# Attention with TensorE's order written out by hand instead of left to the scheduler

## The chip, the cores and the metric

One core of a Trainium2 chip runs the whole kernel. The metric is the device time of one execution in microseconds (us), from the first to the last instruction of the program and what little lies around them. The engines are TensorE (PE: matmuls and transposes; PEld is its loading of weights), VectorE (DVE), ScalarE (ACT), GpSimd (POOL) and SyncE (SP, which here issues the DMAs). Each engine works through its own list of instructions in a fixed order; an instruction whose input is not there yet holds up everything behind it on that engine.

## What is computed

One layer of a trunk with 1024 frames of 1024 channels, in float32 (the matmul operands are split in a high and a low part, and a product is three matmuls, so that it keeps the precision). Only the attention matters here:

```python
x = x + 0.5 * swiglu(rmsnorm(x))
h = rmsnorm(x)
[a | q | k | v | gate logits] = h @ w_in
yA = gMLP spatial gating of gelu(a)
# yB: stick-breaking attention, 16 heads of 64 channels, strictly causal, blocks of 128 frames
z = q_block @ k[:kend].T * scale                     # kend = 128 * (block + 1)
log_keep = where(causal, -softplus(z), 0)
log_w = log_sigmoid(z) + reverse_cumsum(log_keep) - log_keep
out = where(causal, exp(log_w), 0) @ v
m = sigmoid(gA) * (yA @ W_A) + sigmoid(gB) * (yB @ W_B)
x = x + m @ W_out
x = x + 0.5 * swiglu(rmsnorm(x)); y = rmsnorm(x)
```

## The kernel before

The program runs in stages: a first feed-forward block, the attention with its projections (its first scores start at 740.1 us, its last product with v at 1266.7 us), the gated branch `gmlp` with the gates and the merge, and a second feed-forward block. Within a stage most of the order is not written in the code: a scheduler places the instructions of all engines at build time, by its own estimate of when each would be ready. The lists it makes are fixed; nothing is reordered on the chip. A block `manual_schedule(engines={PE})` keeps TensorE's instructions in the order of the code; in the attention before the change only the first projection of v stands in such a block.

**The work of one head** (`head`, line 601 on; 16 heads, two to a pair). The head has eight blocks of 128 queries, b = 0 to 7. For each block TensorE makes the scores `z` in PSUM (tag `p0`, three buffers) from `q` and from `kh` and `kl`, the two parts of k, in pieces of at most 512 keys; ScalarE makes two sigmoids of them, `kp` (what is kept) and `bt`; GpSimd masks the diagonal (`affine_select`); VectorE runs a reversed product scan over the whole row of `kp` (128 to 1024 elements, longer for later blocks); GpSimd, and for the second half of long rows VectorE, multiplies `bt` by it. Two blocks make a step c = 0 to 3. For a step TensorE transposes the weights in groups of two key blocks (`tr`, PSUM tag `p2`, two buffers: 1, 2, 3 and 4 groups in steps 0 to 3), ScalarE and VectorE split each group into a high and a low part (`wt`, by `split`), and TensorE multiplies them with v into `av` (the first product of a group needs the high part, the second the low one). After steps 1 and 3 ScalarE copies `av` to `y` and two DMAs write it out.

**The projections.** `proj_v` makes v for four heads (a quad) in products of 24 matmuls of 256 columns (`pv`); `proj_qk` makes q and k for a pair, each in two halves of 24 matmuls of 512 columns (`pj`). Both use PSUM tag `p1`, two buffers. ScalarE and VectorE split the results. The parts of k are then copied to the other 64 partitions by DMA, and scores need the original and the copy. The tiles of q, `kh` and `kl` have three buffers each, two of which a pair uses. Weights come by DMA into `raw`, ScalarE makes the high part (`wf`, line 56) and VectorE the low part (line 57).

The code calls the two heads of a pair, then the projections for the next; the scheduler moves the projections between the steps of the heads as their buffers allow. The first four products of gate logits (`GAT = 4`, dictionary `ga`) come after the attention in the code, and their tiles are of a pool that is open by then, so the scheduler uses them in the last pair of heads.

Of the kernel before, what the change touches and what calls it, by code (L numbers as in the profile page):

```python
# [24 lines left out]
GAT = 4  # L25
# [7 lines left out]
class Kernel:  # L33
# [525 lines left out]
    def attention(self, ap, ydram):  # L559
        nc, w_in = self.nc, self.a["w_in"][0]  # L560

        def proj_v(quad):
            units = [self.load_cols(w_in, C_VV + quad * 256, kt0, 4, 256) for kt0 in (0, 4)]
            vt = []
            for t in range(NT):
                if quad == 0 and t and self.pending:
                    self.pending.pop(0)()
                half, c = t // 4, (t % 4) * P
                ps = self.psum("p1", "pv")
                for k in range(NK):  # L570
                    wh, wl = units[k // 4]
                    hh, hl = (self.h[half][part][:, k, c:c + P] for part in range(2))
                    self.mm3(ps[:, :256], hh, hl, wh[:, k % 4, :], wl[:, k % 4, :], k == 0, k == NK - 1)
                pool = ap if quad % 2 else self.gp
                v = pool.tile([P, 4, 2, HD], F32R, tag="v", bufs=8, name="v")
                self.split(v[:, :, 0, :], v[:, :, 1, :], ps[:, :256].rearrange("p (h d) -> p h d", h=4))
                vt.append(v)
            return vt

        def proj_qk(pair):  # L580
            lo, hi = slice(0, HD), slice(HD, P)
            kl = [ap.tile([P, S], F32R, tag="kl", bufs=3, name="kl") for _ in range(2)]
            q = [ap.tile([P, S], F32R, tag="q", bufs=3, name="q") for _ in range(2)]
            kh = [ap.tile([P, S], F32R, tag="kh", bufs=3, name="kh") for _ in range(2)]
            wh, wl = self.load_cols(w_in, C_Q + pair * P)
            for half in range(2):
                cs = slice(half * HALF, (half + 1) * HALF)
                ps = self.proj_t("p1", wh, wl, half)
                for e, (own, other) in enumerate(((lo, hi), (hi, lo))):
                    self.split(q[e][own, cs], q[e][other, cs], ps[own, :])  # L590
            wh, wl = self.load_cols(w_in, C_K + pair * P)
            for half in range(2):
                cs = slice(half * HALF, (half + 1) * HALF)
                ps = self.proj_t("p1", wh, wl, half)
                for e, (own, other) in enumerate(((lo, hi), (hi, lo))):
                    self.split(kh[e][own, cs], kl[e][own, cs], ps[own, :])
                    for k in (kh[e], kl[e]):
                        nc.sync.dma_start(out=k[other, cs].bitcast(F32), in_=k[own, cs].bitcast(F32))
            return [(q[e], kh[e], kl[e]) for e in range(2)]

        def head(hd, q, kh, kl, vt):
            hq = hd % 4
            for c in range(4):
                if c % 2 == 0:
                    av = self.psum("p3", "av")
                wts = []
                for b in (2 * c, 2 * c + 1):
                    kend = (b + 1) * P
                    kp = ap.tile([P, S], F32, tag="kp", bufs=KPB, name="kp")
                    bts = []  # L610
                    for s0 in range(0, kend, HALF):
                        n = min(HALF, kend - s0)
                        z = self.psum("p0", "z")
                        nc.tensor.matmul(z[:, :n], lhsT=q[:, b * P:(b + 1) * P], rhs=kh[:, s0:s0 + n], start=True, stop=False)
                        nc.tensor.matmul(z[:, :n], lhsT=q[:, b * P:(b + 1) * P], rhs=kl[:, s0:s0 + n], start=False, stop=True)
                        bt = ap.tile([P, HALF], F32, tag="bt", bufs=BTB, name="bt")
                        nc.scalar.activation(kp[:, s0:s0 + n], z[:, :n], AF.Sigmoid, scale=-(HD ** -0.5))
                        nc.scalar.activation(bt[:, :n], z[:, :n], AF.Sigmoid, scale=HD ** -0.5)
                        bts.append(bt)
                    dk = kp[:, b * P:kend]  # L620
                    db = bts[-1][:, (b % 4) * P:(b % 4 + 1) * P]
                    for d, fill in ((dk, 1.0), (db, 0.0)):
                        nc.gpsimd.affine_select(d, d, pattern=[[-1, P]], compare_op=ALU.is_gt, fill=fill, base=0, channel_multiplier=1)  # L623
                    rev = kp[:, 0:kend][:, ::-1]
                    nc.vector.tensor_tensor_scan(rev, rev, rev, 1.0, op0=ALU.mult, op1=ALU.bypass)  # L625
# [6 lines left out]
                for j0 in range(0, 2 * c + 2, 2):  # L632
# [3 lines left out]
                    for jj in range(2):  # L636
                        j = j0 + jj
                        for bb in range(2):
                            if diag and jj == 1 and bb == 0:
                                continue  # L640
# [23 lines left out]
        for pair in range(npair):  # L664
# [4 lines left out]
            if pair + 1 < npair:  # L669
                qk[pair + 1] = proj_qk(pair + 1)  # L670
# [250 lines left out]
```

## Time and profile before

| | us |
|---|---|
| median of three runs (2529.93 to 2532.69) | 2530.52 |
| the profiled execution's own time | 2532.02 |
| its span, first to last instruction | 2530.3 |
| busy: TensorE | 2455.8 (97%) |
| busy: VectorE | 1675.4 (66%) |
| busy: ScalarE | 1045.0 (41%) |
| busy: GpSimd | 341.9 (14%) |
| mean granted clock of TensorE | 0.984 of full speed |

Busy times of different engines overlap. A busy TensorE need not be a fast one: at half the clock its matmuls take longer and it counts as busy all the same, so the granted clock of a stretch has to be read beside its busy time. The profiled execution took 1.7 us more than its span.

### The profile page before, as it was taken

To read this page: it belongs to the slowest core of one execution; us is meant where nothing else is said; L and a number is where in the kernel's file an instruction comes from. 1 tells how busy PE (TensorE), PEld (TensorE's weight loads), DVE (VectorE), ACT (ScalarE), POOL (GpSimd) and SP (SyncE) were. 2 spreads that over 40 slices of the span, in tenths; PEclk is the share of its full clock that TensorE was granted. 3 is DMA by queue.
4 is the path that set the end of the run, shared out by engine and by line. 5 is a ranking of instruction groups with operands and counts; after the bars stand their busy time and mean duration, and the time that the engine had idled before them with its cause. 6 is when DMAs were issued, how large, how long until landed. Compare 5 with 4: busy or idle time off the path is not lost.

```text
span 2530.3 us, 33327 instructions
## 1 busy us (share of the span) xinstructions
PE 2455.8 (97%) x12268; PEld 2082.9 (82%) x12268; DVE 1675.4 (66%) x2581; ACT 1045.0 (41%) x1994; POOL 341.9 (14%) x508
## 2 busy tenths in 40 slices
PE   7999999999999999999999999999989999999998
PEld 6888888788788888888888988888868888887886
DVE  5777777565747888876666556145757777874655
ACT  6333333354546666665522222232343333333444
POOL 4000000000314444443300000000130000000002
PEclk9999999999999999999999999999999999999999
DMA  5553553785412222221121122133345535547753
GB/s 151 178 171 126 177 176 122 266 290 172 157 51 51 67 51 67 51 67 55 51 53 49 54 76 88 53 101 133 122 147 177 172 130 178 171 138 254 265 174 133
DMA packets 257636, 326.73 MB, mean 129 GB/s; under 512 B 15680, under 2 KB 172864, under 8 KB 257472
## 3 DMA queue, kind: packets, MB, share of 16 engines
q1 hardware_dynamic: 257472, 324.60, 39.7%
q8 instruction: 96, 1.57, 0.3%
q14 instruction: 68, 0.56, 0.1%
HBM read 231.74 MB, written 84.41 MB: 125 GB/s over the span
## 4 chain that ended last, share of the span: by engine, by line
PE 88%; DVE 5%; DMA 3%; issue 1%; ACT 1%; POOL 1%; SPq 0%; DVEq 0%; POOLq 0%; ACTq 0%
PE pd L170 7%; PE pd L172 7%; PE pd L171 7%; PE pj L67 7%; PE pj L68 7%; PE pj L69 7%; PE pb L172 5%; PE pb L171 5%; PE pb L170 5%; PE av L649 3%; PE pv L67 2%; PE pv L68 2%; PE pv L69 2%; PE tr L642 2%; PE pe L171 2%; PE pe L172 2%
## 5 line engine op out<-in xcount | busy, mean ns | idle before, releaser
L154 ACT CAST wf<-raw 128x512 fp32r<-128x512 f32 x280 | 167.2, 620 | 255.7 <-PE pd L172 106.6
L155 DVE TENSOR_TENSOR wf<-raw,wf 128x512 fp32r<-128x512 f32 x264 | 180.2, 702 | 122.9 <-ACT wf L154 122.4
L67 PE MATMUL pj<-h,wf 128*128 128x512 f32 x640 | 255.4, 399 | 5.6 <-DVE q L74 5.6
L68 PE MATMUL pj<-h,wf 128*128 128x512 f32 x640 | 254.7, 398 | 0.0
L69 PE MATMUL pj<-h,wf 128*128 128x512 f32 x640 | 254.0, 397 | 0.6 <-DVE wf L57 0.6
L625 DVE TENSOR_TENSOR_SCAN kp<-kp 128x128 f32<-128x128 f32 (+7 forms) x128 | 178.8, 1406 | 38.4 <-POOL kp L623 36.9
L57 DVE TENSOR_TENSOR wf<-raw,wf 128x1024 fp32r<-128x1024 f32 x88 | 109.5, 1245 | 135.0 <-ACT wf L56 135.0
L154 ACT CAST wf<-ws 128x512 fp32r<-128x512 f32 x176 | 108.0, 622 | 202.2 <-DVE ws L163 106.5
L56 ACT CAST wf<-raw 128x1024 fp32r<-128x1024 f32 x88 | 92.6, 1053 | 219.8 <-PE pj L68 122.2
L67 PE MATMUL pv<-wf,h 128*128 128x256 f32 x512 | 146.9, 289 | 6.9 <-DVE h L74 4.8
L67 PEld LDWEIGHTS pj<-h,wf 128*128 128x128 f32 x640 | 122.8, 192 | 31.5 <-DVE q L74 7.1
L68 PE MATMUL pv<-wf,h 128*128 128x256 f32 x512 | 147.4, 288 | 0.2 <-DVE wf L57 0.2
L69 PE MATMUL pv<-wf,h 128*128 128x256 f32 x512 | 147.1, 288 | 0.0
L629 POOL TENSOR_TENSOR bt<-bt,kp 128x512 f32<-128x512 f32 (+4 forms) x128 | 127.9, 1002 | 138.1 <-DVE kp L625 108.9
L69 PEld LDWEIGHTS pj<-h,wf 128*128 128x128 f32 x640 | 122.4, 191 | 26.0 <-DVE wf L57 1.2
L68 PEld LDWEIGHTS pj<-h,wf 128*128 128x128 f32 x640 | 122.7, 192 | 24.1
L115 POOL TENSOR_TENSOR xn<-x,gain 128x512 f32<-128x512 f32 x12 | 17.2, 1434 | 896.7 <-DVE x L513 601.1
L170 PE MATMUL pb<-T,wf 128*128 128x512 f32 x352 | 137.6, 391 | 0.0
L171 PE MATMUL pb<-T,wf 128*128 128x512 f32 x352 | 137.2, 390 | 0.0
L172 PE MATMUL pb<-T,wf 128*128 128x512 f32 x352 | 137.0, 389 | 0.0
L171 PE MATMUL pd<-wf 128*128 128x512 f32 x344 | 134.4, 392 | 1.3 <-DVE wf L155 1.3
L170 PE MATMUL pd<-wf 128*128 128x512 f32 x344 | 126.7, 401 | 8.3 <-ACT wf L154 8.2
(217 smaller groups left out, 6573.2 us busy)
## 6 DMA issues: line engine op xcount, KB each, us to landing
raw<-in_ff_w_down_dram SPq DMA_DIRECT2D x66, 512.0 KB, 6.2
raw<-in_w_in_dram SPq DMA_DIRECT2D x56, 512.0 KB, 4.1
raw<-in_ff_w_gate_dram SPq DMA_DIRECT2D x52, 512.0 KB, 4.6
raw<-in_ff_w_up_dram SPq DMA_DIRECT2D x44, 512.0 KB, 5.7
f_t2t<-as SPq DMA_DIRECT2D x22, 512.0 KB, 4.8
f_a11a<-act SPq DMA_DIRECT2D x44, 256.0 KB, 4.4
f_s2s<-as SPq DMA_DIRECT2D x22, 512.0 KB, 2.7
f_s3s<-as SPq DMA_DIRECT2D x22, 512.0 KB, 5.8
```

The source lines that it names most:

```text
L56: nc.scalar.copy(hi, raw)
L57: (nc.gpsimd if early else nc.vector).tensor_tensor(lo, raw, hi.bitcast(F32), op=ALU.subtract)
L67: mm(ps, lhsT=lh, rhs=rh, start=first, stop=False)
L68: mm(ps, lhsT=lh, rhs=rl, start=False, stop=False)
L69: mm(ps, lhsT=ll, rhs=rh, start=False, stop=last)
L154: self.nc.scalar.copy(f[:, 0, :], src)
L155: (sub or self.nc.vector.tensor_tensor)(f[:, 1, :], src, f[:, 0, :].bitcast(F32), op=ALU.subtract)
L170: mm(ps, lhsT=lh, rhs=rh, start=first, stop=False, skip_group_check=True)
L171: mm(ps, lhsT=lh, rhs=rl, start=False, stop=False, skip_group_check=True)
L172: mm(ps, lhsT=ll, rhs=rh, start=False, stop=last, skip_group_check=True)
L625: nc.vector.tensor_tensor_scan(rev, rev, rev, 1.0, op0=ALU.mult, op1=ALU.bypass)
L629: eng.tensor_tensor(bt[:, :n], bt[:, :n], kp[:, i * HALF + 1:i * HALF + 1 + n], op=ALU.mult)
```

## The change

All of TensorE's work in the attention goes into one `manual_schedule` block. The projections are cut into units of three matmuls (`product`, `channels`, `v_units`, `q_units`, `k_units`). A list `plan` names, for one head, the pieces of scores (`Z`; `N` for the first two blocks of the next head), the groups of transposes (`T`) and the products with v (`A`) in their order, with numbers between them: shares of the head's projection work (`fill`) that go in at that place. `pair_fill` says which projections each head of a pair carries: the even head q of the next pair and a quarter of a quad's v, the odd head another quarter of v and k of the next pair. Pair 6 carries q and k of the last pair and the first of the four early gate products, pair 7 the other three; their code moves from after the attention into it. q becomes eight tiles of half the length in place of three of the full one, and `y` has one buffer in place of two. `v_units` is called for each pair, so the weights of v of the last three quads are loaded and split twice. The other engines stay with the scheduler, which places them around TensorE's fixed order.

```diff
-GAT = 4
...
+            return [(3 * cols, lambda k=k: unit(k)) for k in range(NK)]
...
-            q = [ap.tile([P, S], F32R, tag="q", bufs=3, name="q") for _ in range(2)]
...
+                        q = out[e, half] = ap.tile([P, HALF], F32R, tag="q", bufs=8, name="q")
+                        self.split(q[own, :], q[other, :], ps[own, :])
...
+        def pair_fill(pair):
+
+            nxt, quad = pair + 1, pair // 2 + 1
+            if nxt == npair:
+                (l1, g1), (l2, g2), (l3, g3) = (gate_units(d) for d in (1, 2, 3))
+                return [l1] + g1[:8] + [l2] + g1[8:] + g2[:8], [l3] + g2[8:] + g3
+            q[nxt], k[nxt] = {}, {}
+            (lq, qs), (lk, ks) = q_units(nxt, q[nxt]), k_units(nxt, k[nxt])
+            if nxt == npair - 1:
+                l0, g0 = gate_units(0)
+                return [lq] + qs[:8] + [l0] + qs[8:] + g0[:8] + [lk], g0[8:] + ks
+            vs = v_units(quad, range(4) if pair % 2 == 0 else range(4, 8), v.setdefault(quad, []))
+            return [lq] + qs[:8] + vs[:1] + qs[8:] + vs[1:17], [lk] + vs[17:] + ks
...
-                    y = ap.tile([P, HALF], F32, tag="y", bufs=2, name="y")
...
+                y = ap.tile([P, HALF], F32, tag="y", bufs=1, name="y")
...
+        plan = [
+            "Z2", .7, "Z3", 1.4, "T0 0", 1.3, "A0 0",
+            "Z4", .4, "Z4", .4, "Z5", .4, "Z5", 1.2, "T1 0", .3, "T1 2", 1.0, "A1 0", .4, "A1 2",
+            "Z6", .4, "Z6", 1.4, "T2 0", .2, "T2 2", .5, "Z7", .6, "T2 4", .2, "Z7", 1.0, "A2 0", .5, "A2 2", .5, "A2 4", 1.8,
+            "N0", .5, "N1", 1.2, "T3 0", .2, "T3 2", .9, "A3 0", .3, "T3 4", .6, "A3 2", .2, "T3 6", .6, "A3 4", .5, "A3 6", .3,
+        ]
+        shares = sum(y for y in plan if not isinstance(y, str))
...
+                if not isinstance(y, str):
+                    asked += y * total / shares
+                    while at < len(fill) and spent + fill[at][0] / 2 <= asked:
+                        spent += fill[at][0]
+                        fill[at][1]()
+                        at += 1
+                    continue
...
-        for pair in range(npair):
-            for e in range(2):
-                head(2 * pair + e, *qk[pair][e], vts[pair // 2])
-            if pair % 2 == 1 and pair + 1 < npair:
-                vts[pair // 2 + 1] = proj_v(pair // 2 + 1)
-            if pair + 1 < npair:
-                qk[pair + 1] = proj_qk(pair + 1)
...
+            for pair in range(npair):
+                for e, fill in enumerate(pair_fill(pair)):
+                    head(2 * pair + e, fill)
...
-            ga = {d: gate(C_GA, 0, d, "p1", True) for d in range(GAT)}
+            ga = self.ga
```

The line numbers of the two programs differ. Below, a row is a line of the code, the operation, what it writes and reads (with the number of each tile) and its shape.

**First place: TensorE in step 1 of head 7 (an odd head), from its first group of transposes to the product with v that needs it.** `tr` are the transposes, `pj` and `pv` projections, `av` the product with v, `z` scores. Before:

```order
L642 MATMUL tr_8629<-ident_66,bt_8607 128x128
L642 MATMUL tr_8629<-ident_66,bt_8620 128x128
L615 MATMUL z_8684<-kl_8166,q_8168 128x256
L614 MATMUL z_8733<-kh_8170,q_8168 128x512
L615 MATMUL z_8733<-kl_8166,q_8168 128x512
L67 MATMUL pj_9100<-h10_83,wf_9067 128x512
...
L69 MATMUL pj_9100<-h10_83,wf_9068 128x512
L614 MATMUL z_8739<-kh_8170,q_8168 128x384
L615 MATMUL z_8739<-kl_8166,q_8168 128x384
L649 MATMUL av_8565<-wt_8596,v_7308 128x256
```

Now:

```order
L727 MATMUL tr_9001<-ident_66,bt_8874 128x128
L727 MATMUL tr_9001<-ident_66,bt_8900 128x128
L66 MATMUL pv_8949<-wf_8614,h10_83 128x256
L67 MATMUL pv_8949<-wf_8615,h10_83 128x256
L68 MATMUL pv_8949<-wf_8614,h11_84 128x256
L727 MATMUL tr_9012<-ident_66,bt_8874 128x128
L727 MATMUL tr_9012<-ident_66,bt_8900 128x128 x2
...
L66 MATMUL pj_9025<-h00_81,wf_8885 128x512
L67 MATMUL pj_9025<-h01_82,wf_8885 128x512
L68 MATMUL pj_9025<-h00_81,wf_8886 128x512
L740 MATMUL av_8937<-wt_9006,v_6444 128x256 x2
```

Between the last transpose of the group and the product that reads its split there stood 18 projection matmuls of 512 columns (the "..." leaves out 16 of them) and scores; now there are six projection matmuls of 256 columns (the "..." leaves out three), three of 512 and the second group's transposes.

**Second place: VectorE's list at the same step.** `kp` are scans of a block's row (640 and 768 wide: blocks 4 and 5; in even heads below, 384 and 512: blocks 2 and 3), `wt` the low parts of the transposed weights, `wf` the low part of projection weights, `bt` a product. Before:

```order
L625 SCALAR_TENSOR_TENSOR kp_8657<-kp_8657 128x640
L629 TENSOR_TENSOR bt_8667<-bt_8667,kp_8657 128x127
L74 TENSOR_TENSOR q_9061<-pj_9071,q_9061 64x512
L74 TENSOR_TENSOR q_9062<-pj_9071,q_9062 64x512
L74 TENSOR_TENSOR wt_8596<-tr_8592,wt_8596 128x384
L74 TENSOR_TENSOR wt_8634<-tr_8629,wt_8634 128x512
L625 SCALAR_TENSOR_TENSOR kp_8677<-kp_8677 128x768
L629 TENSOR_TENSOR bt_8687<-bt_8687,kp_8677 128x255
```

Now:

```order
L706 SCALAR_TENSOR_TENSOR kp_8942<-kp_8942 128x640
L710 TENSOR_TENSOR bt_8956<-bt_8956,kp_8942 128x127
L56 TENSOR_TENSOR wf_9276<-raw_9273,wf_9275 128x1024
L706 SCALAR_TENSOR_TENSOR kp_8969<-kp_8969 128x768
L73 TENSOR_TENSOR wt_9006<-tr_9001,wt_9006 128x512
L73 TENSOR_TENSOR wt_9016<-tr_9012,wt_9016 128x384
```

The split of the first group of step 1 (128x512) stood ahead of the scan of block 5; now it stands behind that scan and a weight split. In the even heads (here head 8) the same stretch, from the scans of blocks 2 and 3 on, now reads:

```order
L706 SCALAR_TENSOR_TENSOR kp_9260<-kp_9260 128x384
L706 SCALAR_TENSOR_TENSOR kp_9283<-kp_9283 128x512
L73 TENSOR_TENSOR kl_9145<-pj_9150,kh_9144 64x512
L73 TENSOR_TENSOR wt_9306<-tr_9302,wt_9306 128x384
L706 SCALAR_TENSOR_TENSOR kp_9317<-kp_9317 128x640
L710 TENSOR_TENSOR bt_9330<-bt_9330,kp_9317 128x127
L73 TENSOR_TENSOR wt_9371<-tr_9366,wt_9371 128x512
L706 SCALAR_TENSOR_TENSOR kp_9340<-kp_9340 128x768
L73 TENSOR_TENSOR wt_9378<-tr_9374,wt_9378 128x384
```

There the split of step 0 (the first 128x384) stands behind the scan of block 3 and a low part of k, and the second split of step 1 behind the scan of block 5.

**Third place: TensorE where the first scores of a new pair (head 8) come.** `pj_9135` (before) and `pj_9025` (now) are the first half of k, which these scores read. Before:

```order
L68 MATMUL pj_9135<-h01_82,wf_9131 128x512
L69 MATMUL pj_9135<-h00_81,wf_9132 128x512
...
L67 MATMUL pj_9168<-h10_83,wf_9131 128x512
L68 MATMUL pj_9168<-h11_84,wf_9131 128x512
...
L642 MATMUL tr_8784<-ident_66,bt_8736 128x128
L642 MATMUL tr_8784<-ident_66,bt_8756 128x128
L69 MATMUL pj_9168<-h10_83,wf_9132 128x512
L614 MATMUL z_9203<-kh_9063,q_9061 128x128
L615 MATMUL z_9203<-kl_9059,q_9061 128x128
```

Now:

```order
L67 MATMUL pj_9025<-h01_82,wf_8885 128x512
L68 MATMUL pj_9025<-h00_81,wf_8886 128x512
L66 MATMUL pj_9150<-h10_83,wf_8885 128x512
L67 MATMUL pj_9150<-h11_84,wf_8885 128x512
L68 MATMUL pj_9150<-h10_83,wf_8886 128x512
L66 MATMUL pj_9150<-h10_83,wf_8885 128x512
L67 MATMUL pj_9150<-h11_84,wf_8885 128x512
L68 MATMUL pj_9150<-h10_83,wf_8886 128x512
L692 MATMUL z_9158<-kh_9138,q_8600 128x128
L692 MATMUL z_9158<-kl_9139,q_8600 128x128
```

Before, all 24 matmuls of k's second half (`pj_9168`) and transposes and products of the heads in hand stood between the end of the first half and the first scores; now six matmuls of the second half do.

## Rows read from the trace of the kernel before

**Rows 1.** By stretches: length, busy PE, PEld, DVE, ACT, POOL (instructions), PEclk, DMA share, GB/s.

```profile
740.00:1267.00 527.00, 511.52 (x3162) 456.62 (x3161) 401.50 (x460) 320.29 (x691) 227.77 (x384) 0.97 0.22 57
764.00:771.00 7.00, 5.29 (x13) 4.14 (x14) 5.77 (x9) 0.38 (x1) 3.93 (x5) 0.51 0.02 4
1269.30:1272.70 3.40, 3.36 (x15) 3.36 (x16) 1.99 (x8) 0.26 (x1) 1.06 (x2) 0.50 0.82 186
```

**Rows 2.** Waits of TensorE, 740 to 1267 us: total us, times, longest.

```profile
PE pj L67 <- DVE q L74: 5.6, 4, 3.1
PE av L649 <- DVE wt L74: 3.9, 5, 1.4
PE tr L642 <- DVE wt L74: 3.0, 2, 1.5
PE av L649 <- ACT y L656: 2.9, 2, 1.7
```

**Rows 3.** The view in order of time, all engines, 855.8 to 861 us.

```profile
856.10 2.28 DVE L625 TENSOR_TENSOR_SCAN kp<-kp 128x1024 f32<-128x1024 f32 x1
856.15 0.39 PE L69 MATMUL pj<-h,wf 128*128 128x512 f32 x1
...
856.57 0.58 ACT L73 CAST kh<-pj 64x512 fp32r<-64x512 f32 x1 [1.18 <-PE pj L69]
856.66 0.62 PE L642 MATMUL tr<-ident,bt 128*128 128x128 f32 x4
857.04 0.48 PE L67 MATMUL pj<-h,wf 128*128 128x512 f32 x1
...
858.02 0.58 ACT L73 CAST wt<-tr 128x512 fp32r<-128x512 f32 x1
...
858.30 0.66 DVE L74 TENSOR_TENSOR kl<-pj,kh 64x512 fp32r<-64x512 f32 x1
...
858.88 0.67 DVE L74 TENSOR_TENSOR wt<-tr,wt 128x512 fp32r<-128x512 f32 x1
858.99 0.59 SPq L598 DMA_DIRECT2D kl<-kl  x1
...
859.55 0.39 PE L67 MATMUL pj<-h,wf 128*128 128x512 f32 x1
...
860.91 0.39 PE L67 MATMUL pj<-h,wf 128*128 128x512 f32 x1
```

**Rows 4.** The view of DMA issues, 740 to 1268 us: KB each, median us to landing.

```profile
kl<-kl SPq DMA_DIRECT2D x30, 128.0 KB, 2.3
```

**Rows 5.** The view by groups, shapes apart, 740 to 1268 us: busy us, mean ns of one.

```profile
L617 ACT ACTIVATE kp<-z 128x512 f32<-128x512 f32 x96 | 59.1, 617 | 20.7 <-PE z L615 19.1 <-POOL bt L629 1.5
...
L623 POOL TENSOR_SCALAR_AFFINE_SELECT kp<-kp 128x128 f32<-128x128 f32 x128 | 46.5, 367 | 176.3 <-ACT kp L617 118.0 <-PE z L615 51.1 <-PE pv L69 5.8
...
L74 DVE TENSOR_TENSOR wt<-tr,wt 128x384 fp32r<-128x384 f32 x64 | 34.9, 546 | 11.7 <-ACT wt L73 11.3
L57 DVE TENSOR_TENSOR wf<-raw,wf 128x1024 fp32r<-128x1024 f32 x26 | 32.5, 1251 | 23.7 <-ACT wf L56 23.7
L625 DVE TENSOR_TENSOR_SCAN kp<-kp 128x896 f32<-128x896 f32 x16 | 32.4, 2023 | 2.1 <-POOL kp L623 2.1
...
L625 DVE TENSOR_TENSOR_SCAN kp<-kp 128x768 f32<-128x768 f32 x16 | 29.2, 1826 | 5.3 <-POOL kp L623 5.2
...
L625 DVE TENSOR_TENSOR_SCAN kp<-kp 128x640 f32<-128x640 f32 x16 | 24.3, 1516 | 4.7 <-POOL kp L623 4.6
L625 DVE TENSOR_TENSOR_SCAN kp<-kp 128x512 f32<-128x512 f32 x16 | 22.0, 1372 | 5.1 <-POOL kp L623 4.4
...
L629 DVE TENSOR_TENSOR bt<-bt,kp 128x127 f32<-128x127 f32 x16 | 12.5, 779 | 2.8 <-POOL bt L623 2.0
...
L617 ACT ACTIVATE kp<-z 128x128 f32<-128x128 f32 x32 | 9.3, 291 | 4.4 <-PE z L615 4.3
```

**Rows 6.** The view in order of time, TensorE, one row after 1269 us.

```profile
1269.34 0.58 PE L67 MATMUL pv<-wf,h 128*128 128x256 f32 x1 [2.10 <-ACT vg L692]
```

More of the change, by code (lines that the diff above doesn't have):

```diff
@@ L560, in attention @@
         nc, w_in = self.nc, self.a["w_in"][0]
[L562 to L571, printed above, removed]
+        lo, hi = slice(0, HD), slice(HD, P)
@@ new lines, in attention, with product, unit, channels @@
+        npair = NHEAD // 2
+        def product(tag, cols, load, step, done):
+            state = {}
+            def unit(k):
+                if k == 0:
+                    state["w"], state["ps"] = load(), self.psum(tag, "pj" if cols == HALF else "pv")
+                step(state["ps"], state["w"], k)
+                if k == NK - 1:
+                    done(state["ps"])
+            return [(3 * cols, lambda k=k: unit(k)) for k in range(NK)]
+        def channels(get, half, done):
+            def step(ps, w, k):
+                self.mm3(ps, w[0][:, k, :], w[1][:, k, :], *(self.h[half][part][:, k, :] for part in range(2)), k == 0, k == NK - 1)
+            return product("p1", HALF, get, step, done)
@@ L660, in attention, with done @@
[L660 to L670 removed]
+                def done(ps):
+                    pool = ap if quad % 2 else self.gp
+                    v = pool.tile([P, 4, 2, HD], F32R, tag="v", bufs=8, name="v")
+                    self.split(v[:, :, 0, :], v[:, :, 1, :], ps[:, :256].rearrange("p (h d) -> p h d", h=4))
+                    out.append(v)
@@ new lines, in v_units, with weights, q_units, done @@
+                units += product("p1", 256, lambda: held["w"], step, done)
+            return units
+        def weights(c0):
+            held = {}
+            return (0, lambda: held.update(w=self.load_cols(w_in, c0))), lambda: held["w"]
+        def q_units(pair, out):
+            load, get = weights(C_Q + pair * P)
+            out.update({(e, half): None for e in range(2) for half in range(2)})
+            def done(half):
+                def run(ps):
+                    for e, (own, other) in enumerate(((lo, hi), (hi, lo))):
+                        q = out[e, half] = ap.tile([P, HALF], F32R, tag="q", bufs=8, name="q")
+                        self.split(q[own, :], q[other, :], ps[own, :])
+                return run
+            return load, channels(get, 0, done(0)) + channels(get, 1, done(1))
```

209 lines of the change are left out of this document (126 added, 83 removed).

## Prediction

> **What bounds the kernel now.** I read the stretches first. From 740 to 1267 us, the sixteen heads, TensorE is busy for 511.5 of 527 us, VectorE for 401.5 and ScalarE for 320.3 [rows 1]. So TensorE sets the pace, and the change neither removes nor adds a matmul there: the same scores, transposes and projections come in another order. What it can win is TensorE's idle time and what the clock loses. The waits give the idle time: 5.6 us for a split of q in four places, 3.9 and 3.0 us for a split of the transposed weights, 2.9 us for the copy of `av`, 15.4 us together [rows 2]. The stretches give the clock: it is granted at 0.97 on average, because of pieces such as that at 764 us, 7 us long at half speed (0.51, the lower of its two levels) [rows 1]. By the mean, 3% of 527 us at half speed or a little less was lost; four pieces of 7 us (one behind each of the four waits for q) at half speed make 14 us. **The most that a better order can win is therefore 15 + 14 = 29 us**, to about 2501.
>
> The Trainium skill ("Perfetto Trace Analysis", "Identifying the Most-Contended Engine") says that matmul busy time is no good measure of TensorE's headroom and points to the busy share of its weight loads. Here that is 456.6 of 527 us, 87%, which would put the headroom at 70 us instead of 29. The trace does not bear that out for this change: a projection matmul starts every 0.23 us without a wait between (below), and another order makes none of them shorter.
>
> The other thing to see is how long VectorE's list is. It is busy for 76% of the stretch, in pieces of up to 2.3 us (the scan of block 7 [rows 3]), and a split that arrives behind a scan waits for all of it.
>
> **What the change adds.** TensorE now meets each result at a place fixed by hand, with little work between. I count what stands between in the new order and set it against the way that the result takes. The steps on TensorE: six projection matmuls in 1.36 us, so 0.227 each [rows 3]; half of it, 0.113, for those of 256 columns and for products with v (an estimate by columns); 0.38 for four transposes, 0.1 each [rows 3]. The hand-overs: a matmul that started at 856.15 ends its step at 856.38 and ScalarE starts at 856.57, 0.2 later; VectorE to the DMA queue took 0.03 [rows 3]; I take 0.05 for each other one. From the end of scores of 512 columns to the start of the scan it is thus 0.2 + 0.62 (sigmoid) + 0.05 + 0.37 (mask) + 0.05 = 1.29 us [rows 5]. Six places in a pair of heads come out short:
>
> First scores of the next pair, odd heads. They need the copy of `kl` on the other partitions. Six projection matmuls stand between, 1.36 us (third place of the order). The way: cast of `kh` from 0.2 to 0.78, low part 0.66, DMA 2.3 us from issue to landing [rows 3, 4]: 3.8 us. Rows 3 show it with a scan of 2.28 us ahead of the low part, just as the new list has it: matmul done at 856.38, DMA issued at 858.99, so landed at 861.3, 4.9 us. The wait is between 2.4 and 3.5 us. In the new order the scores of block 7 end 3.3 us before that half of k (nine projection matmuls and twelve products with v, two of these of 128 columns), so the scan is over at 3.57 of the same count, a product (0.78 taken, [rows 5]) at 4.35, while `kl` could start at 4.1. I take 2.6.
>
> Step 0, even heads. From the end of block 3's scores TensorE has six projection matmuls, three transposes, three projection matmuls and one product: 2.45 us to the product that reads the low part. VectorE: scan of 512 from 1.29 to 2.66, low part of k 0.66, split 0.55, 3.92 with the hand-over [rows 3, 5]. Wait 1.5. Odd heads have no low part of k there and nine half matmuls for six and for three: 3.26 against 2.45, 0.8.
>
> Step 1, odd heads (first and second place). From block 4's second scores to the low product I count 4.55 us. VectorE: 0.96 to the scan (sigmoid of 128: 0.29), scan 1.52, product 0.78, weight split 1.25, scan of block 5 1.83, split 0.67: 7.06 [rows 3, 5]. Wait 2.5. Even heads: the second split is behind the scan of block 5. From the end of the first group of transposes, split done at 1.5, scan 1.83, split 0.55: 3.93 against 2.22. Wait 1.7.
>
> Step 2, both heads. The third group of transposes needs a `p2` buffer, which is free when the first group is split, behind the scan of block 6 (2.02 us [rows 5]): 1.2 + 2.02 + 0.67 + 0.05 = 3.94 against 3.29. Wait 0.6, twice.
>
> A pair waits 2.6 + 1.5 + 0.8 + 2.5 + 1.7 + 1.2 = 10.3 us. In the seven pairs that prepare another one that is 72; the last has no first scores to wait for, 8 more: **80 us**. The bounds: if VectorE had nothing queued, only the 2.4 of the first scores and the bare way of step 0's split would stay (0.2 + 0.58 + 0.55 + hand-overs = 1.4 against 0.8 and 1.1: 0.9 us a pair), 24 us in all. If each of the five other waits met one more short split (0.55) and the first scores the full 3.5, it is 14 a pair, 108 in all.
>
> **The clock.** A single wait of 2.10 us at 1269.34 [rows 6] was followed by 3.4 us at 0.50 [rows 1]: 1.7 us lost. Each odd head has two such waits, 2.5 and 2.6: 15 in all, 26 us. But half a clock on TensorE is time for VectorE, which shortens the next short waits, so I take half, 13. Bounds: 0, and 3.4 us for each (the long piece), 51.
>
> **What it costs nothing.** The four gate products were in this stretch before. q has as many splits; its eight half tiles end the waits for q, counted in the 29. With one `y`, a copy waits for the DMAs of the last one, some 2.3 us [rows 4], and half a head lies between two copies; were that cover gone it would be a wait of that size per copy. Six more loads of v weights cost ScalarE 1 us and VectorE 1.25 each [rows 5]; VectorE has 125 idle us in the stretch, and where one stands in front of a split it is in the sum above.
>
> **Sum.** 80 + 13 - 29 = +64 us on the span of 2530.3. The profiled execution (2532.0) lies 1.5 above the median of the runs, so I put the sum on the median: 2594 us, slower by 2.5%. The corners of the bounds are 2530.5 + 24 - 29 = 2526 and 2530.5 + 108 + 51 - 29 = 2660.
>
> **Rivals.** (a) The order does what it says, faster. The mechanism: VectorE is free when a split arrives, because each wait of TensorE lets it work off its queue, and the first scores' wait is too short to move the clock. Then 24 - 29 = -5, 2525, and down to 2503 if `kl` lands early as well. Against it: the new lists have the scans ahead of the splits by number, and a list is not reordered. It decides where waits and clock together fall under 29 us, 3.6 us a pair; the first scores alone take 2.4 of them. Chance 0.12. (b) The waits only change places: the lower bound with 1.7 us of clock for each of the seven first scores, 24 + 12 - 29 = +7, 2537; a little less of it is no change. Chance 0.10, half of it within 0.2%, which is about what these runs can tell from no change. (c) The clock falls at every group of waits, not at the long ones alone. Before, it fell behind waits that came close together, none over 3.1 us [rows 2]. Four groups a pair at 3.4 us make 109 us in place of 13: 2690. Against it: waits of 1.5 us stand alone in the new order. The Trainium skill ("TensorE: Matmul & The Clock Gate", "A second HAM failure mode: psum-queue depth-cycling") tells of a kernel where small idle times between matmul groups made the clock swing; by that this case is the likely one. Chance 0.10. The forecast has 0.68.
>
> The range that leaves out no more than 2 in 10 goes from 2540 to 2655: below it lie (a) and most of (b), above it (c). Faster by over 0.2%: 0.12; within: 0.05; slower: 0.83.
>
> **What would show it.** Waits of TensorE for `kl`'s DMA at the first scores, seven times 2 to 3.5 us; for `wt` some four or five times a head pair; none for q. The stretch of the heads grows to about 590 us, with VectorE's busy time hardly changed. The granted clock falls under 0.97 with two low pieces a pair. The forecast is wrong if the splits reach TensorE within 1.5 us of their transposes (then (a)), or if TensorE's waits are there and the clock stays at full speed (then some 13 us less).

## The result, and the profile after

The changed kernel took **2644.02 us** (median of four runs, 2641.85 to 2645.52), the kernel before 2530.22 in the same comparison: a ratio of **1.0457, 95% interval 1.0445 to 1.0470**. That is 114 us more where 64 were forecast. The profiled execution has a span of 2643.6 us.

First the stretches, as in [rows 1]: the sixteen heads, and one of the low pieces.

```profile
740.00:1366.00 626.00, 529.05 (x3067) 452.46 (x3065) 421.27 (x464) 332.09 (x695) 285.73 (x384) 0.95 0.20 52
1112.50:1115.90 3.40, 3.40 (x12) 2.92 (x11) 1.60 (x3) 1.67 (x3) 0.00 (x0) 0.50 0.31 79
```

The heads grew from 527 to 626 us. TensorE's instruction count fell a little (3162 to 3067), because gate and `gmlp` products that the scheduler had put between the heads now come behind them. So I compare a longer stretch with the same matmuls on both sides, from the first scores to the first `pa` matmul of `gmlp`: 740.3 to 1299.9 us before, 740.5 to 1414.5 after, 559.6 against 674.0 us. All 114 us are in there. VectorE's busy time in the heads grew by 20 us with four instructions more, GpSimd's by 58 us with the same 384. The prediction had VectorE's hardly changed and did not foresee GpSimd's; it matters below.

The waits of TensorE in the heads, which answer to [rows 2]:

```profile
PE av L740 <- DVE wt L73: 56.3, 37, 2.9
PE z L692 <- DMA kh<-kh: 12.0, 7, 2.2
PE z L692 <- DMA kl<-kl: 8.8, 7, 1.4
PE pv L66 <- DVE q L73: 7.7, 6, 1.5
PE tr L727 <- DVE wt L73: 7.4, 12, 0.9
PE av L740 <- ACT wt L72: 2.5, 7, 0.4
```

The splits of the transposed weights and the DMAs of k head the list, as forecast; the wait for a split of q is a new one. One such wait in the order of time, all engines, step 1 of an odd head (the first place of the order shown ahead of the prediction):

```profile
1103.81 0.28 PE L692 MATMUL z<-kl,q 128*128 128x128 f32 x1
...
1103.92 0.33 PE L66 MATMUL pv<-wf,h 128*128 128x256 f32 x1
...
1105.30 1.55 DVE L706 TENSOR_TENSOR_SCAN kp<-kp 128x640 f32<-128x640 f32 x1 [2.54 <-POOL kp L704]
...
1106.47 0.60 PE L727 MATMUL tr<-ident,bt 128*128 128x128 f32 x4
...
1106.94 1.10 POOL L710 TENSOR_TENSOR bt<-bt,kp 128x512 f32<-128x512 f32 x1 [1.42 <-DVE kp L706]
1106.96 1.23 DVE L710 TENSOR_TENSOR bt<-bt,kp 128x127 f32<-128x127 f32 x1
...
1107.02 0.28 PE L67 MATMUL pv<-wf,h 128*128 128x256 f32 x1
...
1107.14 0.28 PE L68 MATMUL pv<-wf,h 128*128 128x256 f32 x1
...
1107.48 1.00 ACT L72 CAST wt<-tr 128x512 fp32r<-128x512 f32 x2
...
1108.11 1.31 DVE L56 TENSOR_TENSOR wf<-raw,wf 128x1024 fp32r<-128x1024 f32 x1
...
1108.29 1.27 POOL L704 TENSOR_SCALAR_AFFINE_SELECT bt<-bt 128x128 f32<-128x128 f32 x1
...
1108.63 0.28 PE L740 MATMUL av<-wt,v 128*128 128x256 f32 x1
...
1109.34 1.83 DVE L706 TENSOR_TENSOR_SCAN kp<-kp 128x768 f32<-128x768 f32 x1
...
1111.10 1.12 DVE L73 TENSOR_TENSOR wt<-tr,wt 128x512 fp32r<-128x512 f32 x2
...
1111.81 1.23 PE L740 MATMUL av<-wt,v 128*128 128x256 f32 x7 [2.90 <-DVE wt L73]
```

ScalarE starts on the transposes at 1107.48, and VectorE's split of them starts only at 1111.10, behind a product, the low part of a weight and a scan, and TensorE stands still for 2.90 us. This is the list that the prediction read off, row by row. One row has another size: the product of 127 columns took 1.23 us where 0.78 was put in.

### The profile page after: what moved, and what is told of

Same layout as the page of the kernel before. It is cut to its first block, busy times and chain, and to the rows that moved or that the text cites. A ratio compares the mean times of both kernels' runs of the same rounds, so it can differ in the third digit from the quotient of the medians.

```text
span 2643.6 us, 33268 instructions
## 1 busy us (share of the span) xinstructions
PE 2488.1 (94%) x12268; PEld 2091.4 (79%) x12268; DVE 1698.4 (64%) x2587; ACT 1059.1 (40%) x2000; POOL 401.2 (15%) x508
## 3 DMA queue, kind: packets, MB, share of 16 engines
q8 instruction: 96, 1.57, 0.3%
## 4 chain that ended last, share of the span: by engine, by line
PE 74%; DVE 9%; issue 7%; POOL 4%; DMA 3%; ACT 2%; SPq 0%; POOLq 0%; DVEq 0%; ACTq 0%
PE pd L169 7%; PE pd L171 7%; PE pd L170 7%; PE pb L171 4%; PE pb L170 4%; PE pb L169 4%; PE pj L66 4%; PE pj L67 4%; PE pj L68 4%; DVE kp L706 3%; POOL bt L704 2%; PE pv L66 2%; PE pv L67 2%; PE pv L68 2%; PE pe L170 2%
## 5 line engine op out<-in xcount | busy, mean ns | idle before, releaser
L66 PE MATMUL pj<-h,wf 128*128 128x512 f32 x640 | 262.7, 411 | 0.5 <-ACT wf L55 0.5
L68 PE MATMUL pj<-h,wf 128*128 128x512 f32 x640 | 255.0, 399 | 1.0 <-DVE wf L56 1.0
L67 PE MATMUL pj<-h,wf 128*128 128x512 f32 x640 | 255.9, 400 | 0.0
L56 DVE TENSOR_TENSOR wf<-raw,wf 128x1024 fp32r<-128x1024 f32 x94 | 117.9, 1255 | 132.8 <-ACT wf L55 132.8
L55 ACT CAST wf<-raw 128x1024 fp32r<-128x1024 f32 x94 | 99.2, 1055 | 217.5 <-PE pj L67 120.4
L740 PE MATMUL av<-wt,v 128*128 128x256 f32 (+1 forms) x640 | 108.2, 290 | 58.8 <-DVE wt L73 56.3
L740 PEld LDWEIGHTS av<-wt,v 128*128 128x128 f32 x640 | 94.9, 193 | 80.6 <-DVE wt L73 66.6
L67 PEld LDWEIGHTS pj<-h,wf 128*128 128x128 f32 x640 | 123.9, 194 | 19.5
L170 PE MATMUL pd<-wf 128*128 128x512 f32 x344 | 134.3, 392 | 0.8 <-DVE wf L154 0.8
```

Of the source, the lines that this page charges most:

```text
L55: nc.scalar.copy(hi, raw)
L56: (nc.gpsimd if early else nc.vector).tensor_tensor(lo, raw, hi.bitcast(F32), op=ALU.subtract)
L66: mm(ps, lhsT=lh, rhs=rh, start=first, stop=False)
L67: mm(ps, lhsT=lh, rhs=rl, start=False, stop=False)
L68: mm(ps, lhsT=ll, rhs=rh, start=False, stop=last)
L170: mm(ps, lhsT=lh, rhs=rl, start=False, stop=False, skip_group_check=True)
```

## The experiments

A table first. The idle and low columns are TensorE's in the stretch from the first scores to the first `pa`: the time in which it works on nothing, with the number of its waits over 0.15 us, and the time at the lower clock level, with the number of unbroken pieces. The distance is counted from the lists, not measured: the work that TensorE's list has between a group of transposes and its first product with v, at the durations used in the prediction, as median and least of 160 groups.

| kernel | us (median) | ratio to before, interval | idle us (waits) | low us (pieces) | distance us |
|---|---|---|---|---|---|
| before | 2530.22 | | 17.8 (15) | 30.7 (5) | 4.6, 0.8 |
| changed | 2644.02 | 1.0457 (1.0445 to 1.0470) | 97.4 (80) | 58.0 (16) | 1.9, 0.7 |
| e1, k first | 2603.64 | 1.0301 (1.0286 to 1.0316) | 75.8 (70) | 13.7 (4) | 1.9, 0.7 |
| e2, transposes first | 2600.55 | 1.0294 (1.0279 to 1.0310) | 69.4 (72) | 41.0 (8) | 3.2, 1.2 |
| e3, both | 2563.37 | 1.0141 (1.0126 to 1.0156) | 50.7 (69) | 3.4 (1) | 3.2, 1.2 |
| e4, free order | 2504.60 | 0.9919 (0.9902 to 0.9935) | 8.2 (11) | 3.4 (1) | 4.9, 1.3 |
| e5, q halves alone | 2506.82 | 0.9922 (0.9910 to 0.9935) | 8.4 (8) | 6.8 (1) | 4.8, 0.6 |
| e6, longer distances | 2557.85 | 1.0116 (1.0101 to 1.0132) | 36.8 (45) | 10.2 (2) | 2.6, 1.4 |
| e7, free order, k first | 2517.26 | 0.9961 (0.9948 to 0.9973) | 13.6 (8) | 10.2 (3) | 4.9, 1.3 |
| e8, pipelined | 2537.29 | 1.0038 (1.0025 to 1.0052) | 26.6 (28) | 6.8 (1) | 3.8, 2.7 |
| e9, products off VectorE | 2612.56 | 1.0337 (1.0322 to 1.0351) | 81.4 (83) | 30.7 (9) | 1.9, 0.7 |
| e10, e8 with that | 2517.56 | 0.9963 (0.9949 to 0.9976) | 12.4 (13) | 3.4 (1) | 3.8, 2.7 |

The theory, as it stood after the result: TensorE meets results at places that the written order puts too close behind their makers. The main rival: VectorE has to work off its list anyway, so that a change of places only changes which wait is seen. A second rival: something beside the order (one `y` buffer, v in two parts, gates late) costs.

**e1: k first.**

```diff
-            return [lq] + qs[:8] + vs[:1] + qs[8:] + vs[1:17], [lk] + vs[17:] + ks
+            return [lq] + qs[:8] + vs[:1] + qs[8:] + vs[1:17], [lk] + ks + vs[17:]
```

The pair before the last, which has gates in place of v, is changed in the same way.

> In the odd heads the projection of k for the next pair comes ahead of the four v blocks, so that both copies of k land long before the first scores of the next pair. Theory (TensorE waits where the order reaches a result early): the waits for the copies of kh and kl, 12.0 and 8.8 us over seven pairs in the changed kernel, end, with one low piece of the clock a pair (3.4 us at half speed, 1.7 us lost): 21 + 12 + some 3 us for the restart after 14 waits, so 2608 us, 2600 to 2620. Rival (VectorE has its list to work off anyway and the waits only change places): the waits for the copies are gone, those for wt and v grow by as much, 2635 to 2646 us.

Measured: 2603.64, in the theory's range. The waits for the DMAs are gone; those for `wt` fell a little, and one for a split of k came up at the projection's bank. The first rows of its view of waits:

```profile
PE av L740 <- DVE wt L73: 47.0, 40, 1.8
PE tr L727 <- DVE wt L73: 12.5, 14, 1.0
PE pv L66 <- DVE q L73: 7.3, 6, 1.5
PE pv L66 <- DVE kl L73: 6.3, 6, 1.0
```

Idle time fell by 21.6 us, and 44 us less at half speed give back 22: together a little more than the 40.4 us gained. More low pieces went than the one a pair that was expected, for the edit did more than move k on TensorE. It also moved VectorE's list: the weight split that stood ahead of the split of step 1 in the odd heads, and the low part of k ahead of that of step 0 in the even heads, now stand elsewhere, and the longest wait that repeats is 1.4 us.

**e2: transposes first.**

```diff
-            "Z2", .7, "Z3", 1.4, "T0 0", 1.3, "A0 0",
-            "Z4", .4, "Z4", .4, "Z5", .4, "Z5", 1.2, "T1 0", .3, "T1 2", 1.0, "A1 0", .4, "A1 2",
+            "T0 0", .3, "Z2", .7, "Z3", 1.4, "A0 0", 1.0,
+            "Z4", .4, "Z4", .4, "T1 0", .3, "T1 2", .4, "Z5", .4, "Z5", 1.2, "A1 0", .4, "A1 2", .6,
...
```

> The transposes of each step stand ahead of the last scores whose scan would come before their split in VectorE's list, and the products stand where they were or later; k as in the changed kernel. Theory (splits behind scans): the waits of TensorE for wt, 56 us before the products and 7 us before the third transposes, fall to under 20 us, and with them one of the two low pieces of the clock a pair: 44 + 12 + 7 us less, about 2580 us, 2560 to 2600; the waits for the copies of k, 21 us, stay. Rival (the waits only change places): the splits come earlier, but the transposes now wait for the scans and the multiplications behind them, idle time stays within 15 us of 97 us and the time within 2625 to 2650 us.

Measured: 2600.55, 0.6 us above the theory's range and twenty above its middle. The splits are no longer late: 0.2 us of waits for `wt` before the products are left of 56.3. But each transpose now comes sooner behind its scan:

```profile
PE tr L727 <- POOL bt L710: 33.0, 43, 3.8
PE z L692 <- DMA kl<-kl: 22.2, 14, 1.9
PE pv L66 <- DVE q L73: 6.6, 6, 1.1
PE z L692 <- DMA kh<-kh: 6.2, 7, 1.3
```

So the rival has half of it: about half of the 64 us of waits for `wt` came back as waits for GpSimd's product `bt`. A distance lengthened on one side of the transposes was taken from the other side. The waits for the copies of k, which were to stay at 21 us, rose to 28.

**e3: both edits.**

> Both edits together. Theory: they act on different waits and add up: 36 + 63 us less, about 2545 us, 2520 to 2570, with TensorE idle under 25 us in the stretch of the heads. Rival (waits only change places): over 2600 us.

Measured: 2563.37, within the theory's range. The two effects add up (40 and 43 us alone, 81 together). Idle time is 50.7 us, twice the expected, 36.8 of it at the transposes, for `bt`. These are 53 waits, one of 3.9 us at the very start, which is followed by the only low piece, and the others of at most 1.3. Behind that piece the clock stays up:

```profile
746.00:1330.00 584.00, 537.41 (x3330) 469.56 (x3329) 440.31 (x520) 340.45 (x712) 241.13 (x383) 1.00 0.24 59
```

**e4: the order left to the scheduler.**

```diff
         with self.tc.manual_schedule(engines={mybir.EngineType.PE}):
...
-            for b in range(2):
-                begin(0, b)[1].pop(0)()
-            for pair in range(npair):
-                for e, fill in enumerate(pair_fill(pair)):
-                    head(2 * pair + e, fill)
+        for b in range(2):
+            begin(0, b)[1].pop(0)()
+        for pair in range(npair):
+            for e, fill in enumerate(pair_fill(pair)):
+                head(2 * pair + e, fill)
```

> The changed kernel with the order of TensorE in the heads left to the scheduler, as before; q in half tiles, v in two parts, one y buffer and the place of the gates in the program stay as changed. Theory (the written order is what costs): the time falls back to that of the kernel before or a little under it, 2515 to 2540 us, and the q waits (5.6 us before) are gone. Rival (the cost comes from what changed beside the order: one y buffer, v weights loaded twice, gates late): over 2580 us.

Measured: 2504.60, 10 us below the theory's range and faster than the kernel before by 0.8%. **The written order alone costs 139 us**, and the second rival falls: one `y`, v in two parts and the late gates cost nothing that shows. The waits for q are not quite gone (4.7 us, now at the projection's bank), but the clock stays up:

```profile
737.00:1276.00 539.00, 530.74 (x3383) 478.36 (x3381) 431.95 (x533) 342.28 (x725) 235.28 (x392) 1.00 0.26 67
```

**e5: q in half tiles, and nothing else, in the kernel before.**

```diff
-            q = [ap.tile([P, S], F32R, tag="q", bufs=3, name="q") for _ in range(2)]
+            q = [[ap.tile([P, HALF], F32R, tag="q", bufs=6, name="q") for _ in range(2)] for _ in range(2)]
...
```

The lines left out pick the half where q is written and read.

> The kernel before with q in half tiles (six of half the size, the same bytes) and nothing else changed; TensorE's order stays the scheduler's. Theory (the written order costs 114 us, and the half tiles gain what the prediction counted for the waits for q): 5.6 us of waits and four low pieces of 3.4 us lost end, about 19 us less than before, 2500 to 2515 us. Rival (the splits of q are late whatever the tiles, or the half tiles gain nothing): 2520 to 2532 us.

Measured: 2506.82, within the theory's range. The half tiles are the whole gain of e4. The 21.7 us are near what the prediction put down for the waits for q and the clock behind them (5.6 + 14), but by luck in the parts: more than half of the waits for q are still there,

```profile
PE pj L67 <- DVE q L74: 3.3, 3, 1.3
```

while idle time fell by 9.4 us, most of it waits for `wt` and for the copy of `av`, and the low pieces by 23.9 us, of which half or a little less is gained.

**e6: longer distances.** The plan of e2 with the transposes one chunk of scores or some projection units later, k first, and the fill as projection half, block of v, projection half, block of v.

```diff
...
-            "Z4", .4, "Z4", .4, "T1 0", .3, "T1 2", .4, "Z5", .4, "Z5", 1.2, "A1 0", .4, "A1 2", .6,
+            "Z4", .4, "Z4", .6, "Z5", .4, "T1 0", .3, "T1 2", .2, "Z5", 1.2, "A1 0", .4, "A1 2", 1.2,
...
-                return [lq] + qs[:8] + vs[:1] + qs[8:] + vs[1:17], [lk] + ks + vs[17:]
+                return [lq] + qs[:8] + vs[:9] + qs[8:] + vs[9:17], [lk] + ks[:8] + vs[17:25] + ks[8:] + vs[25:]
```

> The order written by hand once more, with k first as before in these experiments, each projection half followed by a block of v, so that no block waits for the projection's bank, and the transposes one chunk of scores or some more projection units further behind their scans. Theory (the written order costs nothing but short distances): the 37 us of waits for the multiplications fall to under 15 us and the 12 us of waits for the splits of q and k end, so TensorE idles under 25 us, no low piece of the clock is left, and with 0.18 us of restart for each wait the time is about 2530 us, 2515 to 2545. Rival (an order of units of three matmuls with transposes between costs by itself, or the waits change places again): over 2555 us.

Measured: 2557.85, the rival's number. The waits for the banks are gone and those for `bt` down to 4.5 us, but 25.6 us for `wt` before the products are back: with the products where they were, the distance is short again (2.6). I read it so that the waits trade places in a head whose products follow in the same step, not that a written order must do so.

**e7: free order, k first.** The fill of e6 in the kernel of e4.

> The order left to the scheduler, with half tiles of q, and in the program k ahead of v in the odd heads and a block of v behind each half of a projection. Theory (with the order free, TensorE has 8 us of waits left, 4.7 of them for splits of q): at most these 5 us are to be had, 2496 to 2506 us. Rival (the place of k and v in the program moves the splits against the scans and brings new waits): over 2512 us.

Measured: 2517.26, 13 us worse than e4; the rival's case. The waits for q went, but 6.0 us for `wt` (one of 2.9) and 5.2 for low parts of k came, with two more low pieces. So a long median distance does not say everything: what stands in VectorE's list at that moment still counts.

**e8: pipelined.** Each group of transposes is followed by another group, and only then by its products; the last product of a head (`P3 6`) stands in the next head, and blocks 2 and 3 (`N2`, `N3`) are scored a head ahead. The fill is that of e6.

```diff
...
+            "T0 0", .3, "Z4", .4, "Z4", .8, "P3 6", .4, "Z5", .4, "Z5", .4,
+            "T1 0", 1.0, "A0 0", .8, "T1 2", 1.0, "A1 0", .4, "Z6", .4, "Z6", .4,
+            "T2 0", 1.0, "A1 2", .8, "T2 2", .2, "Z7", .3, "Z7", .6, "A2 0", .8, "T2 4", 1.0, "A2 2", 1.0,
+            "N0", .3, "N1", .6, "T3 0", 1.0, "A2 4", .8, "T3 2", .6, "N2", .6, "A3 0", .6,
+            "T3 4", .6, "N3", .6, "A3 2", .6, "T3 6", 1.0, "A3 4", .8,
...
```

> An order written by hand in which each group of transposes is followed by another group, and only then by its products; the last product of a head stands in the next head's first step, and the scores of blocks 2 and 3 are made a head ahead. Counted in work that the order places on TensorE between a group of transposes and its first product, the median is 3.8 us and the least 2.7, against 1.9 and 0.7 in the changed kernel, 4.6 and 0.8 in the one before. Theory (only the distance decides, written order or not): TensorE idles under 15 us in the stretch of the heads, and the time falls to that of the free order with q in halves, 2505 to 2525 us. Rival (units of three matmuls with transposes and scores between them cost by themselves, or the scheduler knows something that a list does not): above 2540 us.

Measured: 2537.29, between the two: 107 us of the 139 are back, with idle time at 26.6 us, not under 15. Of that, 16.9 us are still for `wt`:

```profile
PE av L740 <- DVE wt L73: 16.9, 18, 1.7
```

**e9 and e10: products off VectorE.** The changed kernel, and e8, with all products of `bt` on GpSimd.

```diff
-KPB, BTB, WTB, DVB = 3, 6, 3, 4
+KPB, BTB, WTB, DVB = 3, 6, 3, 8
```

> The changed kernel with its four products of bt and kp a head that VectorE makes (127, 255, 383 and 511 columns) given to GpSimd, so that GpSimd makes all of them; TensorE's order stays as written. In the changed kernel these products took 1.22, 0.46, 0.85 and 1.60 us on VectorE, 66 us in all, since they start while GpSimd makes its own product of 512 columns; alone the same ones took 0.29 to 0.68 in the trace of before. Theory (the splits are late because of what VectorE's list holds ahead of them, and the forecast took 0.78 for a product that always takes 1.22 there): the wait of step 1 in the odd heads falls from 2.9 to about 1.7 us, that of step 2 is gone, idle TensorE falls by 15 to 25 us with one low piece of the clock a pair less, 2600 to 2625 us. Rival (the distances alone decide and the products' place doesn't matter, or GpSimd becomes late and the transposes wait for it): 2635 us or more.

> The pipelined order with the same products given to GpSimd. Theory: its 16.9 us of waits for wt before the products with v fall by half, 2525 to 2533 us. Rival (GpSimd, with four products more a head, is late for the transposes): 2540 us or more.

Measured: 2612.56 for e9, in the theory's range, with 16 us less idle time and 27 us less at the low clock. The wait of step 1 in the odd heads became two, 0.87 and 1.48 us, together 2.35 and not 1.7: without the product, the scan of block 5 stands between the two splits. The wait at the third transposes, which was to go, stayed (10.3 us for 7.4); gone is that of step 1 in the even heads. And the waits for `kl` at the first scores, 8.8 us in the changed kernel, are down to 3.0, since the product of 511 columns no longer stands ahead of the low part of k:

```profile
PE tr L727 <- DVE wt L73: 10.3, 16, 1.1
...
PE z L692 <- DMA kl<-kl: 3.0, 7, 0.5
```

For e10 2517.56, below the theory's range; its waits for `wt` are down from 16.9 to 4.1 us. **An order written by hand is thus faster than the kernel before, by 0.4% (0.24 to 0.51%)**, but 13 us slower than the free order with q in halves (e4), and level with that order under the same fill (e7, 2517.26). Whether the free order gains too from products off VectorE was not run. The stretches and waits of e10:

```profile
739.00:1290.00 551.00, 538.62 (x3389) 474.34 (x3387) 381.06 (x469) 340.10 (x725) 328.58 (x456) 1.00 0.25 65
```

```profile
PE av L740 <- DVE wt L73: 4.1, 4, 1.9
PE pj L66 <- DVE kl L73: 3.8, 6, 0.6
```

## Why the prediction was right, and where its sizes were off

**The mechanism held.** There are waits at all six places that the prediction named, behind the rows that it named (at the third transposes 0.9 us in the even heads, and in the odd ones 0.2 or none), and changing the places gives the time back step by step (e1 to e3, e8), the order as a whole all of it (e4). In one pair (1047 to 1126 us), forecast and measured, in us:

| place | forecast | measured |
|---|---|---|
| first scores, odd heads | 2.6 | 2.95 (1.61 + 1.34) |
| step 0, even | 1.5 | 2.46 (0.35 + 2.11) |
| step 0, odd | 0.8 | 1.27 |
| step 1, odd | 2.5 | 2.90 |
| step 1, even | 1.7 | 1.38 |
| third transposes, twice | 1.2 | 0.94, once |
| v block, for the split of q | none | 1.18 |
| sum | 10.3 | 13.1 |

**The accounts.** In the stretch with equal matmuls, 114.4 us are 79.6 more of waits (17.8 to 97.4), some 13.6 more lost to the clock (low pieces from 30.7 to 58.0 us, half of which is lost), and 21.2 of neither. (TensorE idled for 4.1 us of the low pieces of before and 0.9 of those after; without them the last two are 15.3 and 19.5.) The forecast had 65 (80 less the 15 that end), -1 (13 less 14) and nothing. Three terms were mis-sized, all to the same side:

*The waits, 80 forecast, 97 measured.* The step that failed first is "a product (0.78 taken, [rows 5])", put in for the products of step 1 and of the first scores. It is the mean of the product of 127 columns over two kinds. In the trace of before, beside GpSimd and alone (VectorE's rows, in order of time):

```profile
752.70 1.22 DVE L629 TENSOR_TENSOR bt<-bt,kp 128x127 f32<-128x127 f32 x1
789.85 0.28 DVE L629 TENSOR_TENSOR bt<-bt,kp 128x127 f32<-128x127 f32 x1
```

The written order repeats one moment sixteen times, and for the products of 127 and 511 columns it is always the long kind; for that of 255 it is the short one in 15 of 16 (458 ns on average, against 1079 before). The groups of the changed kernel, shapes apart, from the lists of VectorE and of GpSimd:

```profile
L710 DVE TENSOR_TENSOR bt<-bt,kp 128x511 f32<-128x511 f32 x16 | 25.7, 1604 | 1.9
...
L706 DVE TENSOR_TENSOR_SCAN kp<-kp 128x512 f32<-128x512 f32 x16 | 25.2, 1574 | 11.2 <-POOL kp L704 11.2
...
L710 DVE TENSOR_TENSOR bt<-bt,kp 128x127 f32<-128x127 f32 x16 | 19.5, 1220 | 1.7
```

```profile
L704 POOL TENSOR_SCALAR_AFFINE_SELECT bt<-bt 128x128 f32<-128x128 f32 x128 | 124.0, 969 | 4.6
```

With 1.22 in place of 0.78 the wait of step 1 in the odd heads comes to 2.94; 2.90 was measured. So close an agreement is luck: the scan of block 4 started 1.38 us behind the scores (1103.92 to 1105.30) where 0.96 was put in, and TensorE's own way took 4.83 us (to 1108.75) and not 4.55. The wait is also there in the first six odd heads alone; in the last two, where no weight split stands ahead of the scan, it is 1.4 us, as in the even heads. At the first scores the product has 511 columns and took 1.60 us; with it off VectorE (e9) the two waits there come to 2.1 us in place of 2.95.

The scan of 512 elements, 1.57 against 1.37 in [rows 5], is such a mean as well. In most even heads it stands just behind GpSimd's product of 383 columns (GpSimd's row and then VectorE's):

```profile
1063.08 0.86 POOL L710 TENSOR_TENSOR bt<-bt,kp 128x383 f32<-128x383 f32 x1
```

```profile
1063.14 1.88 DVE L706 TENSOR_TENSOR_SCAN kp<-kp 128x512 f32<-128x512 f32 x1 [0.37 <-POOL kp L704]
```

In head 2 it took 1.22 us, and the wait for the low part in step 0 was 1.45 us there, not 2.1. The other 0.35 us of that place are a wait for the high part, which stood behind a cast of k on ScalarE. The other failed step is "q waits end": the wait for q's tiles ended, but a block of v now asks for the PSUM bank of the second half of q while its split is queued. That is 7.7 us in all, and 4.7 in e4.

*The clock, 13 forecast, 29 lost.* The count, two low pieces a pair, came out, 16 in the heads, but in part by luck: 10 stand behind the two places that the forecast named, five behind step 0 of the even heads, where it had a wait of 1.5 us and no piece, and one at the start. "So I take half" was wrong. The reason given, that VectorE catches up during a slow piece, may be so, but waits and clock both came out above their terms: no relief shows, and 15 pieces at the full 1.7 us and one twice as long make 29. The 14 us to be gained were too many as well: TensorE idled in part of those pieces, and the 30.7 us at the low level before cost 13.3 with the piece behind the heads, 11.6 without it. Rival (c), a piece of twice the length for each of four groups a pair, is refuted by the count here and by e3, where 69 waits left one piece. What it had right is that two waits close together can count as one: the first scores' 1.6 and 1.3 us, with one matmul between them, were followed by a piece in six of seven pairs, while of the six single waits of 2.9 us four were.

*What no wait shows, 0 forecast, 21 measured.* A wait costs more than its row. In the timeline of step 1 a matmul of 256 columns is 0.28 us long, and where nothing is awaited the next one starts 0.12 after it (1107.02, 1107.14). The product behind that of 1108.63 would thus have started at 1108.75 and started at 1111.81, 3.06 us later; its row counts 2.90, from the end at 1108.91, and the other 0.16 are overlap that is lost. 65 more waits make some 10 us (an estimate from these numbers). Another 4 us stand at the first projection matmuls behind transposes and short products (below). About 7 us stay open.

**What was put at nothing** is borne out by e4 in the scheduler's order: gates, `y`, the six more loads of v weights; in the written one no wait for `y` shows either. **Of the 29 us of possible gain** the half tiles alone bring 22 (and e4 in all 23 against its own runs of the kernel before). Rivals (a) and (b) fell with the result. (a)'s mechanism, that VectorE is free when a split arrives, did not hold: TensorE waited 64 us for VectorE's splits of the transposed weights. One bound of (a) does not come out of its terms: with `kl` early as well, 24 less the 17 of the first scores less 29 gives 2509, not 2503. It changes neither the range nor a chance.

## What to carry to other kernels

Before writing out an order for one engine, count for each result the work that stands between its maker and its user, and set it against the other engines' lists as they will stand at that moment; where the list of the engine between is long, the user belongs a whole group later, not a few matmuls. A mean duration is the price of an operation only where its moments stay mixed: an order that repeats one moment fixes one of the cases (here the bad one for two of four products), so look whether the rows behind the mean fall into two kinds. And try the parts of a change apart: here a gain of 22 us from half tiles of q lay under a loss of 139.

## What the runs showed of the hardware

**VectorE and GpSimd block each other by whole instructions.** The changed kernel, GpSimd's rows and then VectorE's, both in order of time:

```profile
1042.41 0.29 POOL L704 TENSOR_SCALAR_AFFINE_SELECT kp<-kp 128x128 f32<-128x128 f32 x1 [1.24 <-ACT kp L694]
1042.83 2.28 POOL L704 TENSOR_SCALAR_AFFINE_SELECT bt<-bt 128x128 f32<-128x128 f32 x1
1045.11 1.09 POOL L710 TENSOR_TENSOR bt<-bt,kp 128x512 f32<-128x512 f32 x1
```

```profile
1042.73 2.29 DVE L706 TENSOR_TENSOR_SCAN kp<-kp 128x1024 f32<-128x1024 f32 x1
1045.14 1.60 DVE L710 TENSOR_TENSOR bt<-bt,kp 128x511 f32<-128x511 f32 x1
```

A mask of 0.29 us takes 2.28 because it starts 0.10 behind a scan of 2.29 and ends 0.09 behind it; a product on VectorE that starts 0.03 behind GpSimd's takes 1.60. In these rows whoever starts second waits for all of the other's instruction. GpSimd's rise of 58 us in the heads is this: its masks of `bt` took 969 ns on average. The Trainium skill ("SBUF — State Buffer", "Who interferes with whom") says that a VectorE instruction with two inputs in SBUF contends with GpSimd's reads and that the one issued first blocks the other fully. The trace agrees: the scans read `kp` twice and the products two tiles, all in SBUF, and the 18 masks of `bt` in the changed kernel that met only splits from PSUM took 0.29 us each.

**A projection matmul behind transposes takes a little longer.** The first projection matmul behind a group of transposes starts 0.31 us ahead of the next one, not 0.23:

```profile
1062.35 0.49 PE L727 MATMUL tr<-ident,bt 128*128 128x128 f32 x3
1062.60 0.48 PE L66 MATMUL pj<-h,wf 128*128 128x512 f32 x1
1062.91 0.39 PE L67 MATMUL pj<-h,wf 128*128 128x512 f32 x1
1063.14 0.40 PE L68 MATMUL pj<-h,wf 128*128 128x512 f32 x1
```

There are 63 such places in the changed kernel and 29 in the one before, 3 us; behind a product with v of 128 columns it is 0.06 us more at 17 places, 1 us. Why is not shown.

**The clock.** The low pieces in the heads of the changed kernel are 3.4 us long at half speed (the lower level, 1.2 GHz), one of them 6.8. But for one at the start and one behind 1.45 us, they stand behind its longest waits: those of 2.1 and 2.9 us, and the two at the first scores, 2.95 together. In e3 the clock stayed at its upper level through 46 us of waits, none over 1.4 us. In e1 two of some twenty waits of 1.4 us were followed by a piece. Which of two equal waits is followed by one these runs don't settle.
